# Block 1 with its late convolution tiles behind the scans, its scan tables earlier, and all four FFNs opened on three outputs

## The chip, the cores and the metric

The kernel runs on one core of a Trainium2 chip. The time is device microseconds of one execution on that core; of several executions the median is given. Within the core the engines run beside each other, each in its own fixed order of instructions: PE (matrix products), DVE (elementwise and scans), ACT (activations and casts), POOL (elementwise), SP (which issues the transfers). A wait in one engine's order holds all that stands behind it there.

## What is computed

Two blocks on 512 positions of width 1024, in float32. The first is a hybrid layer: a projection, a gated depthwise convolution of 31 taps over 1024 channels with a layer norm, beside it a state-space layer (S5), gates, an output projection. The second has two layers, each FFN, mixer, FFN; the mixer is a convolution with RWKV in the first ("even") and attention in the second ("odd").

```python
proj = einsum("bld,de->ble", rms_norm(x, pre_g), w_in)
conv_in, z_c, u_s, z_s, g_c, g_s = split(proj)
ca, cb = split(conv_in, 2)
cu = causal_depthwise_conv(ca * sigmoid(cb), conv_w, conv_b)      # 31 taps, per channel
cu = silu(layer_norm(cu, ...))
conv_out = (cu * silu(z_c)) @ w_conv_out
y = gelu(s5_mimo(u_s, ...))          # s_t = Abar s_{t-1} + Bbar u_t;  y_t = Re(C s_t) + D u_t
y = y * sigmoid(y @ w_glu + b_glu)
ssm_out = (y * silu(z_s)) @ w_ssm_out
merged = sigmoid(g_c) * conv_out + sigmoid(g_s) * ssm_out
x = x + rms_norm(merged @ w_out, post_g)
for layer in range(2):
    x = x + 0.5 * swiglu(rms_norm(x, g[0]), w_gate[layer, 0], w_up[layer, 0], w_down[layer, 0])
    x = x + (conv_rwkv if layer == 0 else attention)(rms_norm(x, g[1]))
    x = x + 0.5 * swiglu(rms_norm(x, g[2]), w_gate[layer, 1], w_up[layer, 1], w_down[layer, 1])
```

## The kernel before

**Products.** Activations lie in eight tiles of 128 channels by 512 positions. Each operand of a float32 product is split into a high and a low part, and PE does three products: high by high (L248), high weight by low activation (L249), low weight by high activation (L250). `wload` (L227) brings a weight piece of 128 by 1024: SP issues the transfer into `raw` (two buffers), ACT casts `wh` (L236, three buffers), DVE subtracts to get `wl` (L237, three buffers; POOL does it in the even mixer). `mm3` (L242) runs over the eight k tiles.

**Block 1** is a string of steps, `ORDER_A` and `ORDER_B` (L999 to L1001), which the body reads left to right. A scheduler then fixes each engine's order of instructions from that priority and from when it reckons operands to be there; class "c" is put back by 20000. A letter is a kind of step and the digit its tile or group:

- p: projection pair of a convolution tile with gating; `vb` (L699), `ca` (L701), `cu` (L708). P: the same for tiles 1, 2, 4, 6, whose convolution PE does; it writes `cp` (L720), ACT casts `cph` (L726), DVE subtracts `cpl` (L727). t: that convolution, 96 products of 256 columns (L743 to L745). c: a convolution on DVE (tiles 5 and 7, one L767 and thirty L770 each) or on POOL with ACT (tiles 0 and 3, `cw` L764 and L765).
- T: the S5 tables (`s5_tables`), some eighty small DVE operations (most by the helper at L366), a few of ACT and POOL. R: rotations (L507 to L512).
- Q, K: `s5_pre` for group q. POOL's outer products make `t1` and `w2` (L530, L533); PE transposes `t1` (L544) and multiplies `w2` (L553); SP writes `tz` row block by row block (L559). `t1` has a single buffer, so POOL's next group waits for PE's transposes; the others have two.
- q, r, x, w: `s5_main` in four parts, with the scan (L594) in the second and `sh` (L603) in the third, and PE's `py` (L608, L609) in the fourth.
- u, s, z, g: projections to u, z_s, z_c and the gates. y, G, L, S, C: gelu, GLU, layer norm (it begins with PE's sum over `sacc`, L847), the two outputs.

Tiles 5 and 7 are issued after the instruction named by `P.last_dve`, and tiles 0 and 3 after `P.last_gp`:

```python
def conv(k):
    with tc.issue_after((P.last_gp if k in CONV_POOL else P.last_dve).ins):
        conv_(k)
```

**FFN.** `ffn` (L297) runs over two halves of eleven pairs of outputs (gate and up), each from one weight load of 2048 columns, and then eight down projections. In the first FFN alone (`cols=HALVES`) the first two pairs are taken apart: three outputs are accumulated together, k by k, and the fourth follows from a weight piece of its own. The reciprocal `rs` (L286) of the norm is needed only by DVE's reading of the first output.

Of the kernel before, what the change touches and what calls it, by code (L numbers as in the profile page):

```python
# [11 lines left out]
ALU = mybir.AluOpType  # L12
PSUM = bass.MemoryType.PSUM
T = 512
# [281 lines left out]

def ffn(P, L, j, nxt, out=None, cols=()):  # L297
    nc, tc = P.nc, P.tc
    gu, dn = P.ap["ffn_gu"][L * 2 + j], P.ap["ffn_dn"][L * 2 + j]
    rs = P.rs  # L300
    P.use_banks(mm=7, sd=1)
    with tc.tile_pool(name=f"f{L}{j}", bufs=2) as ph, tc.tile_pool(name=f"m{L}{j}", bufs=1) as mp:
# [3 lines left out]
        acc = None  # L306
        first = []
        if cols:
            w0, w1 = P.wload(gu[0], 2048), P.wload(gu[1], 1024)
            pss = [P.ps() for _ in range(4)]  # L310
            for s in cols:
                for k in range(8):
                    for ps, (h, l), o in ((pss[0], w0, 0), (pss[1], w0, 1024), (pss[2], w1, 0)):
                        P.mm3(ps[:, s], h, l, o + 128 * k, [P.xh[k][:, s]], [P.xl[k][:, s]], k == 0, k == 7)
            h, l = P.wload(gu[1][:, 1024:], 1024)
            P.mm3(pss[3], h, l, 0, P.xh, P.xl)
            first = [pss[0:2], pss[2:4]]
        for hh in range(2):
            for f in range(11):
                if first:  # L320
                    pg, pu = first.pop(0)
                else:
                    h, l = P.wload(gu[hh * 11 + f], 2048)
# [27 lines left out]
def s5_tables(P, mp):  # L351
    nc = P.nc
# [49 lines left out]
    def t9(name):  # L402
        return P.t(name)[:, 0:288].rearrange("p (n g) -> p n g", n=9)

    pr, pi = t9("pr"), t9("pi")
    V.memset(pr[:, 0], 1.0)
# [51 lines left out]
    cmul(pr[:, 5:9], pi[:, 5:9], pr[:, 1:5], pi[:, 1:5], rep(pr[:, 4], 4), rep(pi[:, 4], 4), 4)  # L458
    npi, nspi, spr = small(9), t9("nspi"), small(9)
    V.tensor_scalar(out=npi, in0=pi, scalar1=-1.0, scalar2=None, op0=ALU.mult)  # L460
# [22 lines left out]
    tt(idd, P.ident[0:16, 0:16].unsqueeze(1).to_broadcast([16, 32, 16]), dd.unsqueeze(2).to_broadcast([16, 32, 16]), ALU.mult)  # L483
    prr, nspr = small(8), small(8)
    for j in range(8):
        V.tensor_copy(prr[:, j], pr[:, 7 - j])
        V.tensor_copy(nspr[:, j], nspi[:, 7 - j])
    perm = sm.tile([128, 128], F32, name="perm")
    V.tensor_copy(perm[:, 0:64], P.ident[:, 64:128])
    V.tensor_copy(perm[:, 64:128], P.ident[:, 0:64])  # L490
    return dict(bc=bc, bb=bb, bbs=bbs, idd=idd, prr=prr, nspr=nspr, spr=spr, npi=npi, mg8=mg8, rot=rot, perm=perm)


def s5_rot(P, tb):
    V = P.nc.vector
    c, s = (P.q4.tile([128, 2048], F32, name=n).rearrange("p (g k) -> p g k", g=32) for n in ("rc", "rsn"))
    V.memset(c[:, :, 0:1], 1.0)
    V.memset(s[:, :, 0:1], 0.0)
    ta, tb_ = P.t("ra"), P.t("rb")
    for i in range(6):  # L500
        m = 1 << i
        n = min(32, 512 // m)
        for g0 in range(0, 32, n):
            g = slice(g0, g0 + n)
            cq, sq = (a[:, g].unsqueeze(2).to_broadcast([128, n, m]) for a in tb["rot"][i])
            A, B = (x[:, 0:n * m].rearrange("p (g k) -> p g k", g=n) for x in (ta, tb_))
            V.tensor_tensor(out=A, in0=c[:, g, 0:m], in1=cq, op=ALU.mult)  # L507
            V.tensor_tensor(out=B, in0=s[:, g, 0:m], in1=sq, op=ALU.mult)
            V.tensor_tensor(out=c[:, g, m:2 * m], in0=A, in1=B, op=ALU.subtract)
            V.tensor_tensor(out=A, in0=s[:, g, 0:m], in1=cq, op=ALU.mult)  # L510
            V.tensor_tensor(out=B, in0=c[:, g, 0:m], in1=sq, op=ALU.mult)
            P.last_dve = V.tensor_tensor(out=s[:, g, m:2 * m], in0=A, in1=B, op=ALU.add)  # L512
    tb["cs"] = c, s


def s5_pre(P, tb, q):
    nc = P.nc
# [30 lines left out]
    for hf in range(2):  # L548
# [9 lines left out]
        for j in range(8):  # L558
            nc.sync.dma_start(tz[16 * j:16 * j + 16, 4 * hf:4 * hf + 4, 16 * j:128], kt[:, :, 0:128 - 16 * j])  # L559
    tb[q] = w2, m1, tz  # L560


def s5_main(P, tb, q, u_dram, y_dram):
# [11 lines left out]
    for j in range(8):  # L575
        nc.sync.dma_start(u[16 * j:16 * j + 16], ud[j])

# [24 lines left out]
    V.tensor_tensor(out=st3[:, :, 0:63], in0=st3[:, :, 0:63], in1=c[:, :, 0:63], op=ALU.mult)  # L602
    V.tensor_tensor(out=sh[:, :, 1:64], in0=st3[:, :, 0:63], in1=vr3[:, :, 0:63], op=ALU.subtract)  # L603
    yield
# [353 lines left out]
def proj_first(P, src, xT, sqx):  # L958
# [33 lines left out]
    for a in range(2):  # L992
# [5 lines left out]
         ("w", 1, slice(0, 512)), ("x", 3, None), ("w", 1, slice(512, 1024)), ("x", 4, None), ("x", 5, None), ("x", 6, None), ("x", 7, None))  # L998
ORDER_A = ("p0 P1 p3 t1 u0 u1 T Q0 P2 R0 K0 t2 Q1 c0 q0 K1 s0 r0 P4 x0 q1 Q2 s1 w0 r1 K2 p5 c3 x1 q2 Q3 t4 w1 r2 K3 P6 c5 "  # L999
           "x2 q3 t6 w2 r3 p7 x3 w3 c7")  # L1000
ORDER_B = "z0 z1 z2 z3 y0 g0 g1 g2 y1 y2 y3 g3 G L g4 g5 g6 S0 g7 S1 C0 C1 C2 C3 C4 C5 C6 C7"  # L1001
B1_CLASS = {"c": "C", "t": "V", "R": "T", "T": "T", "Q": "Q", "K": "Q", "q": "S", "r": "S", "x": "S", "w": "S", "y": "S", "G": "S", "L": "L"}
# [1035 lines left out]
```

## Time and profile before

| what | value |
|---|---|
| median of 3 runs | 2653.73 us (2647.78 to 2653.99) |
| the profiled execution's own time | 2650.77 us |
| its span | 2649.0 us |
| granted clock, mean | 0.97 |
| PE busy | 2512.6 us, 95% |
| DVE, ACT, POOL busy | 1474.5, 925.5, 484.2 us |
| chain that ended last | 78% PE, 9% DVE, 3% POOL |

The span is cut into stages by time: block 1 to about 560 us, the first FFN to about 955, the even mixer to about 1320, two FFNs to about 2030, the odd mixer to about 2282, the last FFN. An average over the span says little of a stage; the windows do. In a row of the windows, "PE busy" is the time in which products run, and PEclk the share of full clock that was granted. A wait row names the line that waited and the instruction that released it.

### The profile page before, as it was taken

To read this page: it belongs to the slowest core of one execution; us is meant where nothing else is said; L and a number is where in the kernel's file an instruction comes from. 1 tells how busy PE (TensorE), PEld (TensorE's weight loads), DVE (VectorE), ACT (ScalarE), POOL (GpSimd) and SP (SyncE) were. 2 spreads that over 40 slices of the span, in tenths; PEclk is the share of its full clock that TensorE was granted. 3 is DMA by queue.
4 is the path that set the end of the run, shared out by engine and by line. 5 is a ranking of instruction groups with operands and counts; after the bars stand their busy time and mean duration, and the time that the engine had idled before them with its cause. 6 is when DMAs were issued, how large, how long until landed. Compare 5 with 4: busy or idle time off the path is not lost.

```text
span 2649.0 us, 31923 instructions
## 1 busy us (share of the span) xinstructions
PE 2512.6 (95%) x12724; PEld 2052.6 (77%) x12724; DVE 1474.5 (56%) x1978; ACT 925.5 (35%) x1322; POOL 484.2 (18%) x332
## 2 busy tenths in 40 slices
PE   8687899999999998999899999999999889999999
PEld 7566788878888876787588888888888677788887
DVE  7888868455344469643754344543444766543443
ACT  5253436243222333222332233322223565422221
POOL 2499602020000164331100000100001231100000
PEclk9798899999999998998999999999999989999999
DMA  5222332313232332314132322322324412222323
GB/s 169 80 85 75 92 111 89 127 66 110 87 105 99 113 129 59 74 49 132 41 100 88 107 96 90 102 98 92 105 86 138 113 62 72 70 97 85 106 93 98
DMA packets 116294, 250.94 MB, mean 95 GB/s; under 512 B 44112, under 2 KB 53072, under 8 KB 116144
## 3 DMA queue, kind: packets, MB, share of 16 engines
q1 hardware_dynamic: 116000, 248.68, 29.7%
q8 instruction: 100, 1.64, 0.3%
q14 instruction: 50, 0.41, 0.0%
q10 hardware_dynamic: 144, 0.22, 0.0%
HBM read 234.30 MB, written 13.37 MB: 93 GB/s over the span
## 4 chain that ended last, share of the span: by engine, by line
PE 78%; DVE 9%; POOL 3%; issue 2%; DMA 2%; ACT 2%; SPq 0%; DVEq 0%; ACTq 0%; POOLq 0%
PE bank L248 24%; PE bank L249 24%; PE bank L250 24%; POOL xa L765 1%; DVE wl L237 1%; DMA s<-nd 1%; PE bank L1913 1%; DVE xa L770 1%; PE bank L1270 1%; POOL acc L265 1%; PE bank L1333 0%; ACT wh L236 0%; PE bank L1346 0%; DVE xl L271 0%; PE bank L1406 0%
## 5 line engine op out<-in xcount | busy, mean ns | idle before, releaser
L248 PE MATMUL bank<-xh,wh 128*128 128x512 f32 (+1 forms) x2152 | 836.7, 391 | 13.6 <-ACT xh L977 5.8
L236 ACT CAST wh<-raw 128x1024 fp32r<-128x1024 f32 x448 | 433.3, 968 | 1187.2 <-PE bank L249 852.5
L249 PE MATMUL bank<-xl,wh 128*128 128x512 f32 (+1 forms) x2152 | 838.0, 390 | 4.3 <-DVE xl L947 2.7
L250 PE MATMUL bank<-xh,wl 128*128 128x512 f32 (+1 forms) x2152 | 836.3, 389 | 2.7 <-DVE wl L237 2.7
L237 DVE TENSOR_TENSOR wl<-raw,wh 128x1024 fp32r<-128x1024 f32 (+2 forms) x414 | 482.7, 1166 | 331.8 <-ACT wh L236 329.3
L248 PEld LDWEIGHTS bank<-xh,wh 128*128 128x128 f32 x2152 | 406.8, 190 | 103.1 <-ACT xh L977 6.5
L249 PEld LDWEIGHTS bank<-xl,wh 128*128 128x128 f32 x2152 | 407.9, 190 | 92.1 <-DVE xl L978 4.6
L250 PEld LDWEIGHTS bank<-xh,wl 128*128 128x128 f32 x2152 | 407.8, 189 | 87.7 <-DVE wl L237 3.6
L265 POOL TENSOR_TENSOR acc<-acc,sq 128x512 f32<-128x512 f32 x54 | 90.1, 1669 | 1298.2 <-ACT sq L264 1291.6
L249 PE MATMUL bank<-ml,wh 128*128 128x512 f32 x704 | 273.9, 389 | 0.0
L250 PE MATMUL bank<-mh,wl 128*128 128x512 f32 x704 | 273.9, 389 | 0.0
L248 PE MATMUL bank<-mh,wh 128*128 128x512 f32 x704 | 272.6, 389 | 0.0
L332 DVE TENSOR_TENSOR up<-bank,rs 128x512 f32<-128x512 f32 x88 | 60.8, 691 | 271.5 <-PE bank L250 271.4
L328 DVE TENSOR_TENSOR gp<-bank,rs 128x512 f32<-128x512 f32 x88 | 60.8, 691 | 174.9 <-PE bank L250 174.7
L250 PEld LDWEIGHTS bank<-mh,wl 128*128 128x128 f32 x704 | 132.2, 188 | 27.6
L249 PEld LDWEIGHTS bank<-ml,wh 128*128 128x128 f32 x704 | 132.2, 188 | 27.4
L248 PEld LDWEIGHTS bank<-mh,wh 128*128 128x128 f32 x704 | 132.2, 188 | 27.3
L237 POOL TENSOR_TENSOR wl<-raw,wh 128x1024 fp32r<-128x1024 f32 x34 | 82.9, 2440 | 139.7 <-ACT wh L236 112.7
L765 POOL TENSOR_TENSOR xa<-xa,cw 128x512 f32<-128x512 f32 x60 | 98.0, 1635 | 10.7 <-ACT cw L764 8.1
L340 DVE SCALAR_TENSOR_TENSOR xa<-bank,xa 128x512 f32<-128x512 f32 x64 | 44.3, 692 | 79.5 <-PE bank L250 79.5
L254 ACT CAST mh<-m 128x512 fp32r<-128x512 f32 x88 | 55.1, 626 | 58.5 <-DVE m L334 58.5
L743 PE MATMUL bank<-cph,wh 128*128 128x256 f32 x128 | 41.0, 320 | 32.2 <-ACT cph L726 32.2
(654 smaller groups left out, 2927.8 us busy)
## 6 DMA issues: line engine op xcount, KB each, us to landing
raw<-in_ffn_gu_dram SPq DMA_DIRECT2D x176, 512.0 KB, 3.5
raw<-in_ffn_dn_dram SPq DMA_DIRECT2D x64, 512.0 KB, 3.5
raw<-in_w_in_dram SPq DMA_DIRECT2D x46, 512.0 KB, 3.5
raw<-in_even_in_dram SPq DMA_DIRECT2D x26, 512.0 KB, 3.5
raw<-in_ffn_dn_dram SPq DMA_DIRECT2D x64, 192.0 KB, 2.3
raw<-in_conv_dram SPq DMA_DIRECT2D x16, 512.0 KB, 3.8
xa<-in_xT_dram SPq DMA_DIRECT2D x16, 256.0 KB, 4.1
raw<-in_w_co_dram SPq DMA_DIRECT2D x8, 512.0 KB, 3.3
```

What stands on the lines that cost most here:

```text
L236: nc.scalar.copy(h[:, :m], raw[:, :m])
L237: self.wlo.tensor_tensor(out=l[:, :m], in0=raw[:, :m], in1=h[:, :m].bitcast(F32), op=ALU.subtract)
L248: self.nc.tensor.matmul(ps, h[i][:, s], xh[k], start=a, stop=False)
L249: self.nc.tensor.matmul(ps, h[i][:, s], xl[k], start=False, stop=False)
L250: last = self.nc.tensor.matmul(ps, l[i][:, s], xh[k], start=False, stop=b)
L254: self.nc.scalar.copy(hi, src)
L265: nc.gpsimd.tensor_tensor(out=acc, in0=acc, in1=sq, op=ALU.add)
L328: nc.vector.tensor_tensor(out=gp, in0=pg, in1=rs, op=ALU.mult)
L332: nc.vector.tensor_tensor(out=up, in0=pu, in1=rs, op=ALU.mult)
L340: nc.vector.scalar_tensor_tensor(out=P.x[o], in0=ps, scalar=0.5, in1=P.x[o], op0=ALU.mult, op1=ALU.add)
L743: nc.tensor.matmul(d, h[:, o], xh, start=a, stop=False)
L765: GP.tensor_tensor(out=y, in0=y, in1=w, op=ALU.add)
```

## The change

It has three parts, all in the order of work; the arithmetic and the number of transfers stay.

1. The order: T goes three steps forward, from behind u1 to before t1; P2 goes from behind Q0 to before u0, and s0, P4, t4, s1, P6 and t6 move forward among the S5 steps; and c5 and c7 go from the end of `ORDER_A` into `ORDER_B`, behind z0. `P.last_dve` is set at `sh` instead of at the last rotation, so the DVE convolutions are issued behind the last group's scan.
2. Reversed rows: the sixteen copies that made `prr` and `nspr` in reverse order (L486, L487) go. The tables are used in their own order, and `tz` and `us` are written to rows 112-16j where they went to 16j.
3. Every FFN takes the first four outputs apart; those that gave no `cols` use one slice of all 512 columns.

```diff
-def ffn(P, L, j, nxt, out=None, cols=()):
+def ffn(P, L, j, nxt, out=None, cols=(slice(0, T),)):
...
-        first = []
-        if cols:
-            w0, w1 = P.wload(gu[0], 2048), P.wload(gu[1], 1024)
-            pss = [P.ps() for _ in range(4)]
-            for s in cols:
...
+        w0, w1 = P.wload(gu[0], 2048), P.wload(gu[1], 1024)
+        pss = [P.ps() for _ in range(4)]
+        for s in cols:
+            for k in range(8):
+                for ps, (h, l), o in ((pss[0], w0, 0), (pss[1], w0, 1024), (pss[2], w1, 0)):
+                    P.mm3(ps[:, s], h, l, o + 128 * k, [P.xh[k][:, s]], [P.xl[k][:, s]], k == 0, k == 7)
+        h, l = P.wload(gu[1][:, 1024:], 1024)
+        P.mm3(pss[3], h, l, 0, P.xh, P.xl)
+        first = [pss[0:2], pss[2:4]]
...
-    pr, pi = t9("pr"), t9("pi")
+    pr, pi = small(9), t9("pi")
...
-    npi, nspi, spr = small(9), t9("nspi"), small(9)
+    npi, nspi, spr = small(9), small(9), small(9)
...
-    prr, nspr = small(8), small(8)
-    for j in range(8):
-        V.tensor_copy(prr[:, j], pr[:, 7 - j])
-        V.tensor_copy(nspr[:, j], nspi[:, 7 - j])
...
-    return dict(bc=bc, bb=bb, bbs=bbs, idd=idd, prr=prr, nspr=nspr, spr=spr, npi=npi, mg8=mg8, rot=rot, perm=perm)
+    return dict(bc=bc, bb=bb, bbs=bbs, idd=idd, prr=pr, nspr=nspi, spr=spr, npi=npi, mg8=mg8, rot=rot, perm=perm)
...
-            P.last_dve = V.tensor_tensor(out=s[:, g, m:2 * m], in0=A, in1=B, op=ALU.add)
+            V.tensor_tensor(out=s[:, g, m:2 * m], in0=A, in1=B, op=ALU.add)
...
-            nc.sync.dma_start(tz[16 * j:16 * j + 16, 4 * hf:4 * hf + 4, 16 * j:128], kt[:, :, 0:128 - 16 * j])
+            nc.sync.dma_start(tz[112 - 16 * j:128 - 16 * j, 4 * hf:4 * hf + 4, 16 * j:128], kt[:, :, 0:128 - 16 * j])
...
-        nc.sync.dma_start(u[16 * j:16 * j + 16], ud[j])
+        nc.sync.dma_start(u[112 - 16 * j:128 - 16 * j], ud[j])
...
-    V.tensor_tensor(out=sh[:, :, 1:64], in0=st3[:, :, 0:63], in1=vr3[:, :, 0:63], op=ALU.subtract)
+    P.last_dve = V.tensor_tensor(out=sh[:, :, 1:64], in0=st3[:, :, 0:63], in1=vr3[:, :, 0:63], op=ALU.subtract)
...
-ORDER_A = ("p0 P1 p3 t1 u0 u1 T Q0 P2 R0 K0 t2 Q1 c0 q0 K1 s0 r0 P4 x0 q1 Q2 s1 w0 r1 K2 p5 c3 x1 q2 Q3 t4 w1 r2 K3 P6 c5 "
-           "x2 q3 t6 w2 r3 p7 x3 w3 c7")
-ORDER_B = "z0 z1 z2 z3 y0 g0 g1 g2 y1 y2 y3 g3 G L g4 g5 g6 S0 g7 S1 C0 C1 C2 C3 C4 C5 C6 C7"
+ORDER_A = ("p0 P1 p3 T t1 P2 u0 u1 Q0 t2 R0 s0 K0 P4 Q1 c0 q0 K1 t4 r0 s1 x0 q1 Q2 p5 w0 r1 K2 P6 c3 x1 q2 Q3 t6 w1 r2 K3 p7 "
+           "x2 q3 w2 r3 x3 w3")
+ORDER_B = "z0 c5 c7 z1 z2 z3 y0 g0 g1 g2 y1 y2 y3 g3 G L g4 g5 g6 S0 g7 S1 C0 C1 C2 C3 C4 C5 C6 C7"
```

What the strings make of the engines' orders is seen in three places. The changed kernel's line numbers are lower by six in these rows (L720 is now L714), except for `wload` and `mm3`. The rows give line, operation, output, inputs and size; a count stands for rows alike.

DVE, around pair 2's `vb`. Before:

```order
L487 COPY s5t_820<-nspi 128x32 x4
L473 TENSOR_SCALAR nn<-nn 128x192
L487 COPY s5t_820<-nspi 128x32 x4
L475 SCALAR_TENSOR_TENSOR ang<-nn,ang 128x192 x2
L699 TENSOR_TENSOR vb<-bank_76,rsl 128x512
L701 TENSOR_TENSOR ca<-bank_75,rsl 128x512
L475 SCALAR_TENSOR_TENSOR ang<-nn,ang 128x192
L237 TENSOR_TENSOR wl<-raw,wh 128x1024
L720 SCALAR_TENSOR_TENSOR cp<-vb,ca 64x256 x3
```

Now:

```order
L237 TENSOR_TENSOR wl<-raw,wh 128x1024
L702 SCALAR_TENSOR_TENSOR cu<-vb,ca 128x512
L237 TENSOR_TENSOR wl<-raw,wh 128x1024 x5
L693 TENSOR_TENSOR vb<-bank_76,rsl 128x512
L695 TENSOR_TENSOR ca<-bank_75,rsl 128x512
L237 TENSOR_TENSOR wl<-raw,wh 128x1024
L714 SCALAR_TENSOR_TENSOR cp<-vb,ca 64x256 x4
L721 TENSOR_TENSOR cpl<-cp,cph 128x2x256
```

Ahead of `vb` stood the tables with their copies; now weights stand there, and the last of the tables' rows is the one just ahead of this piece.

DVE, at the convolution of tile 5 and 7. Before, around the `cp` of pair 6:

```order
L237 TENSOR_TENSOR wl<-raw,wh 128x1024
L770 SCALAR_TENSOR_TENSOR xa<-cu,hcw,xa 128x512 x3
L557 TENSOR_TENSOR kt<-kt,idd 16x4x16
L770 SCALAR_TENSOR_TENSOR xa<-cu,hcw,xa 128x512 x2
L699 TENSOR_TENSOR vb<-bank_74,rsl 128x512
L701 TENSOR_TENSOR ca<-bank_73,rsl 128x512
L770 SCALAR_TENSOR_TENSOR xa<-cu,hcw,xa 128x512
L601 TENSOR_TENSOR vr<-bank_79,rsn 128x8x63
L602 TENSOR_TENSOR st_2028<-st_2028,rc 128x8x63
L237 TENSOR_TENSOR wl<-raw,wh 128x1024
L720 SCALAR_TENSOR_TENSOR cp<-vb,ca 64x256 x4
L770 SCALAR_TENSOR_TENSOR xa<-cu,hcw,xa 128x512
```

Now, at the last group's scan and behind it:

```order
L588 SCALAR_TENSOR_TENSOR st_2383<-d_2330,vs 128x512
L237 TENSOR_TENSOR wl<-raw,wh 128x1024
L595 TENSOR_TENSOR vr<-bank_77,rsn 128x8x63
L596 TENSOR_TENSOR st_2383<-st_2383,rc 128x8x63
L597 TENSOR_TENSOR sh<-st_2383,vr 128x8x63
L761 TENSOR_SCALAR xa<-cu,hcw,vec 128x512 x2
L237 TENSOR_TENSOR wl<-raw,wh 128x1024
L764 SCALAR_TENSOR_TENSOR xa<-cu,hcw,xa 128x512 x9
```

The steps of tiles 5 and 7 were strewn through the scans and stood ahead of `cp`; now the first of them (L761) comes after the last `sh`.

PE, at the first transposes of S5 (`t` is `t1`). Before:

```order
L744 MATMUL bank_80<-cpl,wh 128x256
L745 MATMUL bank_80<-cph,wl 128x256
L743 MATMUL bank_80<-cph,wh 128x256
L744 MATMUL bank_80<-cpl,wh 128x256
L544 MATMUL bank_77<-ident,t_840 128x128 x4
L745 MATMUL bank_80<-cph,wl 128x256
```

Now:

```order
L250 MATMUL bank_74<-xh_98,wl 128x512
L248 MATMUL bank_74<-xh_99,wh 128x512
L249 MATMUL bank_74<-xl_107,wh 128x512
L250 MATMUL bank_74<-xh_99,wl 128x512
L538 MATMUL bank_77<-ident,t_898 128x128 x4
L538 MATMUL bank_78<-ident,t_898 128x128 x4
```

The first transposes, at place 418, stood inside the convolution of tile 2 (L743 to L745). They now come at place 530, behind that convolution and behind the projection s0.

## Rows read from the trace of the kernel before

**Rows 1.** Windows of block 1: span, busy time (instructions) by engine, clock, transfers.

```profile
core 0: us, PE busy (x) PEld busy (x) DVE busy (x) ACT busy (x) POOL busy (x), PEclk, DMA share, GB/s
100.00:200.00 100.00, 76.39 (x393) 63.22 (x394) 85.05 (x96) 41.51 (x59) 77.41 (x56) 0.86 0.24 72
200.00:300.00 100.00, 74.24 (x429) 63.36 (x429) 88.25 (x72) 46.30 (x68) 89.15 (x57) 0.81 0.27 78
300.00:400.00 100.00, 99.60 (x454) 82.42 (x453) 71.03 (x88) 37.98 (x51) 15.34 (x11) 1.00 0.33 105
100.00:120.00 20.00, 11.46 (x73) 11.02 (x74) 18.07 (x34) 6.42 (x9) 10.48 (x11) 0.65 0.14 40
260.00:280.00 20.00, 4.85 (x22) 4.37 (x22) 19.78 (x23) 7.45 (x12) 13.49 (x8) 0.50 0.15 42
```

**Rows 2.** PE's waits from 20 to 300 us: total, times, longest.

```profile
PE bank L743 <- ACT cph L726: 32.2, 2, 18.6
```

**Rows 3.** Timeline at the first wait: start, length, instruction [idle before it, and releaser].

```profile
79.98 0.09 DVE L406 MEMSET pr<- 128x32 f32 x1
...
98.33 2.23 DVE L487 COPY s5t<-nspi 128x32 f32<-128x32 f32 x4
...
101.94 0.68 DVE L699 TENSOR_TENSOR vb<-bank,rsl 128x512 f32<-128x512 f32 x1
...
106.18 1.28 ACT L479 ACT_TABLE_LOAD   x1 [2.90 <-DVE ang L476]
...
108.40 0.58 PE L743 MATMUL bank<-cph,wh 128*128 128x256 f32 x1 [18.61 <-ACT cph L726]
```

**Rows 4.** Timeline: a weight subtraction alone, and the second wait.

```profile
69.00 1.21 DVE L237 TENSOR_TENSOR wl<-raw,wh 128x1024 fp32r<-128x1024 f32 x1
...
268.48 2.28 DVE L237 TENSOR_TENSOR wl<-raw,wh 128x1024 fp32r<-128x1024 f32 x1
...
270.69 3.75 DVE L720 SCALAR_TENSOR_TENSOR cp<-vb,ca 64x256 f32<-64x256 f32 x4
...
275.15 0.58 PE L743 MATMUL bank<-cph,wh 128*128 128x256 f32 x1 [13.62 <-ACT cph L726]
```

**Rows 5.** Timeline of DVE beside POOL at 109.8 us.

```profile
109.76 1.27 POOL L533 TENSOR_TENSOR t<-t,tmp 128x512 f32<-128x512 f32 x1
109.80 1.28 DVE L510 TENSOR_TENSOR ra<-rsn,rc 128x32 f32<-128x32 f32 x1
```

**Rows 6.** POOL's stretch: its window, DVE's groups in it, later window of L770 alone.

```profile
117.43:255.98 138.55, 112.92 (x594) 91.79 (x592) 118.34 (x104) 59.69 (x86) 122.16 (x84) 0.91 0.27 77
...
L237 DVE TENSOR_TENSOR wl<-raw,wh 128x1024 fp32r<-128x1024 f32 x17 | 30.2, 1774 | 15.5 <-ACT wh L236 15.5
L770 DVE SCALAR_TENSOR_TENSOR xa<-cu,hcw,xa 128x512 f32<-128x512 f32 x17 | 23.6, 1386 | 0.4
...
340.00:360.00 20.00, 10.19 (x14) 1.00 0.33 109
```

**Rows 7.** Timeline: ends of POOL's stretch, and PE at place 1029 of its order.

```profile
117.43 1.26 POOL L530 TENSOR_TENSOR t<-s5bb,s5t 128x512 f32<-128x512 f32 x1 [1.04 <-PE bank L544]
...
256.04 0.40 PE L553 MATMUL bank<-w,s5bb 128*16 128x128 f32 x1 [2.71 <-POOL w L533]
...
303.33 0.39 PE L249 MATMUL bank<-xl,wh 128*128 128x512 f32 x1
303.56 0.39 PE L250 MATMUL bank<-xh,wl 128*128 128x512 f32 x1
```

**Rows 8.** Timeline of FFN openings; last row: PE's waits from 2280 to 2310 us.

```profile
592.79 0.50 PE L248 MATMUL bank<-xh,wh 128*128 128x512 f32 x1 [0.30 <-ACT wh L236]
...
1334.75 3.35 DVE L286 RECIPROCAL rs<-s 128x512 f32<-128x512 f32 x1 [1.76 <-ACT s L284]
...
PE bank L248 <- DVE xa L1952: 3.9, 1, 3.9
```

More of the change, by code (lines that the diff above doesn't have):

```diff
@@ L306, in ffn @@
         acc = None
-        first = []
-        if cols:
-            w0, w1 = P.wload(gu[0], 2048), P.wload(gu[1], 1024)
-            pss = [P.ps() for _ in range(4)]
-            for s in cols:
[L312 to L317, printed above, removed]
+        w0, w1 = P.wload(gu[0], 2048), P.wload(gu[1], 1024)
[7 more added lines that the diff above has]
+        first = [pss[0:2], pss[2:4]]
         for hh in range(2):
```

## The prediction

> **What bounds the kernel now.** I read the windows first. The reader is to see a kernel whose PE is the bound nearly everywhere, and one stretch where it isn't: from 100 to 300 us PE is busy 76.4 and 74.2 of each 100 us, at a granted clock of 0.86 and 0.81, while the 100 us behind them stand at 99.6 and 1.00 [rows 1]. The worst slices are 100 to 120 us (PE busy 11.5 of 20, clock 0.65) and 260 to 280 us (4.9 of 20, clock 0.50, the lower of the two levels, 1.2 GHz, all through). The list of PE's waits names the cause of both: ACT's cast of cph, 32.2 us in two waits, the longest 18.6 [rows 2].
>
> The timeline shows why the casts are late. First wait: DVE works from 79.98 through the S5 tables, among them small copies in POOL's company (four of 128x32 take 2.23 us), and reaches vb of pair 2 only at 101.94; its cp and cast follow, and tile 2's first product issues at 108.40 after 18.61 us of idleness [rows 3]. Second wait: at 268.48 DVE runs a weight subtraction of 2.28 us that takes 1.21 at 69.00, then four cp that take 3.75, and tile 6's first product waits for their cast until 275.15 [rows 4]. Steps of convolution tiles 5 and 7 (L770) are strewn between, in DVE's order.
>
> Both engines are slow there because they get in each other's way. At 109.80 a DVE operation on 32 columns takes 1.28 us and ends when POOL's 1.27 us one from 109.76 does [rows 5]. From 117.43 to 255.98 POOL is busy 122.2 of 138.6 us; the 17 convolution steps that DVE has there take 1386 ns each, and 0.73 us (10.19 for 14) once POOL is idle [rows 6].
>
> **What the change does, part by part.** *Tables, then P2, ahead.* In the new order the tables of T are done before t1's last weights, and pair 2's vb has six weight subtractions in front of it instead of the tables. So the wait of 18.6 us should go. The tables aren't free: they fall beside t1's weights. ACT gets four table loads of 1.28 us [rows 3] between t1's casts, 5.1 us, and I add 1.4 us for small DVE operations in front of wl: **6.5 us lost**. Bounds: nothing, if the three weight buffers cover it, or 22 us, the time from 79.98 to 101.94 that the tables take DVE now [rows 3], if they all stood in front of a weight.
>
> *When the first S5 transposes come.* PE's order stands at place 386 when the wait for pair 2 begins, 18.61 us before 108.40, at 89.8. The same 386 places hold the same work in the new order; then come t2's 96 products and the 48 of s0, and at place 530 the transposes. At 0.227 us for 512 columns (303.33 to 303.56 [rows 7]) and half of it for 256 these are 10.9 and 10.9 us: 89.8 + 21.8 + 6.5 = **118 us**, taken as 119 for the transposes themselves.
>
> *From there POOL sets the pace.* t of the S5 preparation has one buffer: POOL's outer products for q1 start at 117.43 when PE has read q0's, and PE takes q3's w at 256.04 after a wait for POOL [rows 7]. In between POOL does 73 tensor operations, 1.90 us each with its idle time. In the new order there are 82 up to the same product. Upper bound: 82 x 1.90 = 156 us. Lower: the 18 DVE steps of tiles 5 and 7 in this stretch are gone, and with them at most their own 0.73 us each in which POOL stood: 156 - 13 = 143. I take **146**, near the lower end, since the nine additional operations bring no DVE work along. So PE's last product of q3's preparation comes at 119 + 146 = 265 us. It is place 1029 of PE's new order; before, place 1029 is a projection product that issued at 303.56 [rows 7]. The new order's first 1029 places hold 3 us more PE work (by the two issue times, place by place). Gain: 303.6 + 3 - 265 = **41.6 us**. The recovered clock is in this number, as it is a difference of clock times.
>
> *The tail.* P.last_dve now lies behind q3's sh, so the 62 DVE steps of tiles 5 and 7 start only then. From there to their last one DVE has 73.6 us to do (62 x 0.73 = 45, 13 wl x 1.21 = 16, the rest z, gelu and gates); sacc adds 2.6. PE has 78 us of products between q3's py and the sum over sacc. Margin 2 us. POOL has 16 operations left after q3's w, most of them past when DVE begins, 21 us of PE work later: I take **2 us lost**. In the trace of before one POOL operation held one DVE operation for its whole length [rows 5]; if all 16 did so, 20 us less the margin would be lost, 18 instead of 2. The Trainium skill's "SBUF — State Buffer", section "SBUF: two separate sides", states this as the rule: DVE with two SBUF inputs and GpSimd lock each other out for the whole instruction. The trace agrees for that pair, and less so for the mean of 1386 ns.
>
> *The copies.* Removing 16 copies takes up to 9 us off DVE (2.23 us per four beside POOL [rows 3]). In the new place POOL has little to do, and they would cost little: nothing, beyond what the first step counts. Reversed rows of tz and us change neither number nor size of transfers: nothing.
>
> *The three FFN openings.* ffn(0,1), ffn(1,0), ffn(1,1) now start with three outputs per k, as ffn(0,0) did. There the fourth output's weight came late in three waits, the first 0.30 us [rows 8], 0.8 in all. In ffn(0,1) and ffn(1,0) DVE's new order also has the reciprocal rs in front of that weight. It starts at 1334.75 and takes 3.35 us [rows 8], some 15 after that FFN's first product, and three outputs last 72 x 0.227 = 16.3: it ends 2 us past that. So 2.8 us lost twice and 0.8 once. And ffn(1,1) opens with a wait of 3.9 us for xa [rows 8], which work on three outputs may shorten a little. I take **5 us lost**; bounds 3.9 gained and 12.4 lost (three times 0.8 + 3.35).
>
> **Sum** against the profiled run's own 2650.8 us (span 2649.0): 2650.8 - 41.6 + 2 + 5 = **2616 us**. The median of the runs is 2653.7, 3 us above; I leave the sum where it is.
>
> **Rivals.**
> 1. *POOL isn't that slow.* With less of DVE beside it POOL could need 1.55 us per operation in place of 1.78, between the 1.27 undisturbed [rows 5] and the 122.2/73 = 1.67 busy [rows 6]. q3's preparation ends 18 us earlier: **2598**. Against: weights (1774 ns [rows 6]), rotation and scans stay there.
> 2. *The tables starve t1.* Should all 22 us stand in front of t1's weights, 15.5 more are lost than counted, and POOL starts as much later: **2631**. For it: the tables are serial over DVE and ACT, and both run in order. Against: the order has seven weight subtractions among them.
> 3. *POOL's last operations hold DVE in the tail.* All 16 of them cost 18 instead of 2: **2632**. It is what the lock rule in the Trainium skill's "SBUF — State Buffer" makes of the tail. Against: 17 steps at 1386 ns are less than 0.73 + 1.27 each, so not every step met one.
> 4. *The tail becomes DVE's; slower.* All 62 steps at the 1386 ns that they took beside POOL are 41 us more, the 13 weights at 1774 ns 7 more: 46 past the margin. PE waits for gates and the sum, and loses to the clock what 100 to 120 us shows, 7 of 20, twice. 2650.8 - 41.6 + 46 + 14 + 5 = **2674**. It decides if POOL is at tile 3 through most of the 62 steps, that is if ACT starves POOL or q3's w comes well before sh. Against: 16 operations at 1.67 are 27 us, no more.
> 5. *The change doesn't do what it says:* pair 2's cast is late all the same, because vb waits for its banks or for tanh's table. The first wait stays with its slow clock, 18.6 + 7: **2642**.
>
> **How the numbers follow.** A measurement here tells about 0.3%, 8 us, from no change. Chances: forecast 0.45 (2606 to 2626), rival 1 0.14, rivals 2 and 3 0.12 each, rival 5 0.05, rival 4 0.07, and 0.05 for what I don't see, most of it slower. Range 2592 to 2642: it takes in rivals 1, 2, 3 and 5 and the bounds of the openings around the forecast, and leaves out 4. Faster by over 0.3% (under 2646): 0.83; within: 0.06; slower: 0.11.
>
> **What would show it.** Right: no wait of L743 for cph over 2 us; PE above 17 of 20 us and clock above 0.95 in the slices from 80 to 240; PE's remaining waits on POOL's w and t; q3's last product of the preparation at about 265; no L770 before q3's sh; DVE above 90% from there; gaps of 1 to 3 us some 16 us after each FFN's first product. Wrong: PE waiting for wl or wh between 45 and 80 us (rival 2), for gates, z or sacc between 290 and 370 (3, 4), for cph at 100 (5). The forecast fails as a whole if the time is above 2646, or if the gain lies outside block 1.

## The result, and the profile after

The changed kernel takes 2629.34 us (median of 3 runs, 2629.21 to 2631.49) where the one before took 2653.73: a ratio of 0.9922, with a 95% interval of 0.9903 to 0.9942. The forecast was 2616 within 2592 to 2642. The profiled execution is the run of 2629.34 us, with a span of 2627.6 and a mean clock of 0.973; against the profiled 2650.77 before, the gain is 21.4 us where 34.8 were forecast. From the S5 rotations on, line numbers of the new kernel are 6 lower (L770 is L764, L743 is L737); the helpers up to L286 keep theirs.

PE's waits in the new kernel, 20 to 420 us (total, times, longest):

```profile
PE bank L737 <- ACT cph L720: 11.6, 2, 7.7
PE bank L739 <- DVE wl L237: 5.2, 3, 3.6
PE bank L738 <- DVE cpl L721: 5.0, 3, 2.3
PE bank L547 <- ACT vs L579: 4.2, 1, 4.2
PE bank L547 <- POOL w L527: 3.0, 1, 3.0
...
PE bank L248 <- DVE zc L793: 1.6, 1, 1.6
```

The wait for cph, 32.2 us in two [rows 2], is down to 11.6, and the first of the two, 18.6 us long, is gone altogether: the two that are left are at tiles 4 and 6. In its place stand many small ones. The windows of the new kernel show where:

```profile
core 0: us, PE busy (x) PEld busy (x) DVE busy (x) ACT busy (x) POOL busy (x), PEclk, DMA share, GB/s
40.00:60.00 20.00, 14.09 (x69) 12.43 (x68) 19.79 (x30) 5.68 (x13) 14.38 (x11) 0.84 0.16 51
100.00:120.00 20.00, 20.00 (x135) 18.50 (x134) 15.69 (x34) 8.28 (x10) 1.73 (x4) 1.00 0.59 183
140.00:160.00 20.00, 8.96 (x41) 6.68 (x41) 16.72 (x13) 7.89 (x13) 19.92 (x13) 0.56 0.24 66
220.00:240.00 20.00, 8.32 (x47) 7.61 (x48) 12.06 (x9) 6.54 (x10) 18.76 (x13) 0.69 0.14 38
260.00:280.00 20.00, 20.00 (x108) 15.94 (x106) 11.46 (x10) 10.70 (x16) 19.45 (x16) 1.00 0.26 74
```

The two bad slices of before [rows 1] are full now: 20.00 of 20 at a clock of 1.00 where 11.46 at 0.65 and 4.85 at 0.50 stood. Two new bad slices lie at 40 to 60, where the tables are made, and at 140 to 160 (8.96 of 20 at a clock of 0.56, where the kernel before had 14.60 at 0.91). One is left at 220 to 240, where POOL is busy 18.76 of 20 us and DVE only 12.06. The timeline of the new kernel shows the waits of the second slice and of the third, at tile 6, and the end of the S5 preparation (start, length, instruction, idle before it and releaser):

```profile
142.30 0.57 ACT L549 COPY kt<-bank 16x512 f32<-16x512 f32 x1 [8.40 <-DMA tz<-kt]
...
143.02 1.09 PE L538 MATMUL bank<-ident,t 128*128 128x128 f32 x4 [2.41 <-ACT kt L549]
...
148.27 3.57 PE L547 MATMUL bank<-w,s5bb 128*16 128x128 f32 x16 [4.16 <-ACT vs L579]
...
155.72 0.58 PE L737 MATMUL bank<-cph,wh 128*128 128x256 f32 x1 [3.88 <-ACT cph L720]
...
223.05 0.72 ACT L758 ACTIVATE cw<-cu,hcw 128x512 f32<-128x512 f32 x1 [5.76 <-POOL xa L759]
223.68 1.03 ACT L236 CAST wh<-raw 128x1024 fp32r<-128x1024 f32 x1
224.62 0.63 ACT L694 ACTIVATE vb<-vb 128x512 f32<-128x512 f32 x1
...
224.74 1.65 DVE L237 TENSOR_TENSOR wl<-raw,wh 128x1024 fp32r<-128x1024 f32 x1 [4.20 <-ACT wh L236]
226.32 5.52 DVE L714 SCALAR_TENSOR_TENSOR cp<-vb,ca 64x256 f32<-64x256 f32 x4
...
232.54 0.58 PE L737 MATMUL bank<-cph,wh 128*128 128x256 f32 x1 [7.72 <-ACT cph L720]
...
266.92 1.41 POOL L527 TENSOR_TENSOR w<-w,tmp 128x576 f32<-128x576 f32 x1
...
270.32 1.05 PE L547 MATMUL bank<-w,s5bb 128*16 128x128 f32 x8
```

In the slice at 140 PE waits three times for ACT: 2.41 us for a copy of `kt` that ACT makes only after 8.40 us of waiting for the transfer of `tz`, 4.16 for `vs` and 3.88 for the cast of tile 4. At tile 6 too the chain runs over ACT, which works in order. At 223.05 it makes the next `cw` of tile 3 only after 5.76 us of waiting for POOL; a weight cast and the gate `vb` of tile 6's pair stand behind that. DVE waits 4.20 us for the cast, its four `cp` take 5.52 beside POOL (3.75 before [rows 4]), and PE's product waits for all of it. The marks that the forecast used, in us:

| mark | before | after | shift | forecast shift |
|---|---|---|---|---|
| first S5 transposes on PE | 115.1 | 124.1 | +9.0 | +4 |
| the two products that the forecast took for place 1029 of PE's order | 303.6 | 270.3 | -33.2 | -38.6 |
| sum over sacc (layer norm) | 409.8 | 380.9 | -28.9 | -39.6 |
| rs of ffn(0,0) | 603.7 | 575.3 | -28.4 | -39.6 |
| rs of the even mixer | 948.9 | 921.3 | -27.6 | |
| rs of ffn(0,1) | 1334.8 | 1315.1 | -19.6 | -37 |
| rs of ffn(1,0) | 1690.6 | 1671.3 | -19.3 | |
| rs of the odd mixer | 2050.5 | 2032.9 | -17.6 | |
| rs of ffn(1,1) | 2299.0 | 2276.6 | -22.4 | -34.8 |
| end | 2650.8 | 2629.3 | -21.4 | -34.8 |

The second row doesn't compare one place. Counted as the forecast counts (the first transposes are number 418 before and 530 after), the product at 303.6 is number 1222 of the profiled order of the kernel before, and the last of q3's preparation, at 271.1, is number 1192 of the new one; number 1192 of the kernel before issues at 296.8.

What block 1 gained can be split by the windows from 20 us to the sum over sacc: PE's idle time falls from 60.0 to 37.3 us, and its busy time from 329.8 to 323.6 at a clock that rises from 0.91 to 0.94. Of the 28.9 us 22.7 are waits.

So two things fell short: block 1 gains 28 us and not 40, and the even mixer loses 8 us, in a stage that the change doesn't touch. The odd mixer gives 5 back. The experiments below ask what makes the 28, why it isn't more, and where the 8 went.

### The profile page after: what moved, and what is told of

It is laid out like the page before. It is cut to its first block, busy times and chain, and to the rows that moved or that the text cites. A ratio compares the mean times of both kernels' runs of the same rounds, so it can differ in the third digit from the quotient of the medians.

```text
span 2627.6 us, 31906 instructions
## 1 busy us (share of the span) xinstructions
PE 2513.7 (96%) x12724; PEld 2054.1 (78%) x12724; DVE 1449.1 (55%) x1962; ACT 928.9 (35%) x1325; POOL 477.6 (18%) x332
## 4 chain that ended last, share of the span: by engine, by line
PE 81%; DVE 9%; POOL 3%; DMA 2%; ACT 2%; issue 2%; SPq 1%; DVEq 0%; POOLq 0%; ACTq 0%
PE bank L248 24%; PE bank L250 24%; PE bank L249 24%; DVE wl L237 1%; POOL xa L759 1%; DMA raw<-in_w_in_dram 1%; POOL acc L265 1%; PE bank L1907 1%; PE bank L1264 1%; ACT wh L236 1%; SPq L553 1%; PE bank L1340 0%; PE bank L1327 0%; DMA s<-nd 0%; DVE cp L714 0%
## 5 line engine op out<-in xcount | busy, mean ns | idle before, releaser
L248 PE MATMUL bank<-xh,wh 128*128 128x512 f32 (+1 forms) x2152 | 836.4, 390 | 16.9 <-ACT xh L971 6.0
L248 PEld LDWEIGHTS bank<-xh,wh 128*128 128x128 f32 x2152 | 405.9, 189 | 108.6 <-issue 7.5
L248 PE MATMUL bank<-mh,wh 128*128 128x512 f32 x704 | 272.6, 389 | 0.0
L248 PEld LDWEIGHTS bank<-mh,wh 128*128 128x128 f32 x704 | 132.2, 188 | 27.5
L332 DVE TENSOR_TENSOR m<-up,sg 128x512 f32<-128x512 f32 x88 | 60.9, 692 | 10.5 <-ACT sg L328 2.3
```

Source lines behind the costliest of these rows:

```text
L248: self.nc.tensor.matmul(ps, h[i][:, s], xh[k], start=a, stop=False)
```

## Experiments

The kernel before was run beside each group of experiments on the same chip; its medians were 2649.96 (beside block 1 alone, FFNs alone, early convolutions, late tables), 2651.17 (copies, tile 6, tile 3, tiles 0 and 3) and 2649.43 (the rest). "Low stretch" is the time that the even mixer spends at a clock under 0.9 around its triangular solve, counted in windows of 2 us; it is 18 us in the kernel before and 36 in the new one.

**Which of the three parts.** The block 1 part alone (the FFNs as before), and the FFN part alone:

```diff
-def ffn(P, L, j, nxt, out=None, cols=(slice(0, T),)):
+def ffn(P, L, j, nxt, out=None, cols=()):
...
```

> The changed kernel with the FFNs of before (only the first one opens on three outputs). Theory: the three new openings are worth next to nothing, since in the changed kernel's trace the second and third FFN differ from before by 1.4 and 0.6 us and the last by no wait at all. So 2627 to 2631 us against 2629. Block 1 keeps its 28 us, and the even mixer its stretch at half clock near 1190 us, because its order of work is the changed kernel's. Rival, as forecast: the openings cost 5 us, then 2624. Second rival: an opening is what shortened the odd mixer's wait for ACT (13.2 to 9.6 us); then 2633.

Measured: 2626.69 us (2625.83 to 2629.20), 0.9913 of before (0.9898 to 0.9928).

> The kernel before with all FFNs opened on three outputs, nothing else. Theory: within 2 us of before, 2651 to 2656, the even mixer with the order of before and the short stretch at half clock (16 us, not 32). Rival: openings cost 5 us, 2658. Second rival: they gain 4 us through the odd mixer, 2649.

Measured: 2651.25 us, 1.0006 of before (0.9996 to 1.0015). The FFN openings are worth nothing: +1.3 us alone, up to 2.6 together with the rest. All of the gain is in block 1.

**The late convolutions.** Tiles 5 and 7 go back to their places between the S5 steps, all else as in the new kernel:

```diff
-            V.tensor_tensor(out=s[:, g, m:2 * m], in0=A, in1=B, op=ALU.add)
+            P.last_dve = V.tensor_tensor(out=s[:, g, m:2 * m], in0=A, in1=B, op=ALU.add)
...
-    P.last_dve = V.tensor_tensor(out=sh[:, :, 1:64], in0=st3[:, :, 0:63], in1=vr3[:, :, 0:63], op=ALU.subtract)
+    V.tensor_tensor(out=sh[:, :, 1:64], in0=st3[:, :, 0:63], in1=vr3[:, :, 0:63], op=ALU.subtract)
...
-ORDER_A = ("... w1 r2 K3 p7 x2 q3 w2 r3 x3 w3")    ORDER_B = "z0 c5 c7 z1 ..."
+ORDER_A = ("... w1 r2 K3 c5 p7 x2 q3 w2 r3 x3 w3 c7")    ORDER_B = "z0 z1 ..."
```

> The changed kernel with one part undone: the DVE convolutions may start after the last rotation again, c5 stands behind K3 and c7 at the end of the first string. Theory (POOL sets the pace of the S5 preparation and DVE's two-input work slows it): POOL's stretch from the first transposes to q3's w goes from 1.75 us per operation back to 1.9, 8 to 13 us, and pair 6's cast is late again, so 2638 to 2645. Rival (the tail is what counts: DVE is busy 105.5 of 112.9 us there): the work spread out is better, 2625 or less. Second rival (POOL does not pace PE): no change, 2629.

Measured: 2657.89 us (2654.69 to 2663.57), 1.0034 of before (1.0022 to 1.0045): slower than the kernel before, and 29 us behind the new one. Its waits of PE, 20 to 420 us, and then its windows:

```profile
PE bank L737 <- ACT cph L720: 18.2, 2, 14.3
PE bank L591 <- DVE st L588: 9.2, 1, 9.2
PE bank L739 <- DVE wl L237: 8.6, 4, 3.5
PE bank L547 <- POOL w L527: 5.8, 2, 5.3
```

```profile
220.00:240.00 20.00, 5.50 (x24) 4.52 (x24) 19.82 (x17) 4.29 (x7) 18.86 (x12) 0.60 0.16 43
240.00:260.00 20.00, 11.80 (x74) 11.30 (x74) 19.68 (x18) 8.39 (x12) 16.85 (x10) 0.71 0.12 34
300.00:320.00 20.00, 10.79 (x45) 7.96 (x43) 19.75 (x20) 3.88 (x5) 10.38 (x7) 0.82 0.18 47
```

DVE is full (19.7 to 19.8 of 20) and PE empty. The DVE steps and what they cost beside POOL, 120 to 300 us of this run (count, busy, mean ns), against the same operation late in the new kernel, 294 to 390 us:

```profile
L764 DVE SCALAR_TENSOR_TENSOR xa<-cu,hcw,xa 128x512 f32<-128x512 f32 x32 | 43.7, 1367 | 0.7
```

```profile
L764 DVE SCALAR_TENSOR_TENSOR xa<-cu,hcw,xa 128x512 f32<-128x512 f32 x60 | 43.0, 754 | 0.0
```

The same step takes 1367 ns beside POOL and 754 ns after it. The mean mixes two kinds (shortest, median and longest of the 32, in ns):

```profile
L764 DVE SCALAR_TENSOR_TENSOR xa<-cu,hcw,xa x32: 730/1636/1878, 208.1 to 298.7; 128x512 f32<-128x512 f32 x32
```

Ten of them take 730 to 752 ns and 22 take 1470 to 1878, with none between, and each of the 22 ends 0.50 to 0.55 us after a POOL operation does. The two other parts of the new order (tables ahead, no copies) gain nothing while the convolutions stay early.

**The tables.** T goes back behind u1:

```diff
-ORDER_A = ("p0 P1 p3 T t1 P2 u0 u1 Q0 ..."
+ORDER_A = ("p0 P1 p3 t1 P2 u0 u1 T Q0 ..."
```

> The changed kernel with T behind u1 again, everything else kept. Theory (POOL's pace counts from the first transposes on): the waits of 7.5 us and the lower clock (0.84 from 40 to 60 us) in tile 1's convolution vanish, about 10 us, but the tables then run at 80 to 105 us and POOL has q0's products ready only at about 120, where the transposes would have been anyway: 2624 to 2631. Rival (PE alone limits from there): the full 10 us are gained, 2619. Second rival (the tables stand in front of pair 2's operands as before): the wait of 18 us is back, 2645 or more.

Measured: 2636.81 us (2633.95 to 2637.66), 0.9951 (0.9934 to 0.9967). The sum over sacc comes at 393.8, 13 us later than in the new kernel; the total shows only 7.5 of that, since the stage of the low stretch is 8.0 us shorter (16 us at the low clock instead of 36). The first product of tile 2's convolution issues at 89.9 us, where it is 101.8 in the new kernel: that is what tables ahead cost PE up to there. The wait of 18.6 us doesn't come back. In this order P2 still stands ahead of the tables, so the wait goes with P2's place and not with the tables' own (P2 alone was not moved in any run). The delay spreads over waits of 11.0 us (L547 for ACT's `vs`), 7.8 (`zc`), 7.5 (L547 for ACT's `m`) and 6.5 (cph). So tables ahead are worth some 13 us in block 1, net of what they cost t1.

**The copies.** The 16 copies and forward rows come back:

```diff
+    prr, nspr = small(8), small(8)
+    for j in range(8):
+        V.tensor_copy(prr[:, j], pr[:, 7 - j])
+        V.tensor_copy(nspr[:, j], nspi[:, 7 - j])
...
-            nc.sync.dma_start(tz[112 - 16 * j:128 - 16 * j, 4 * hf:4 * hf + 4, 16 * j:128], kt[:, :, 0:128 - 16 * j])
+            nc.sync.dma_start(tz[16 * j:16 * j + 16, 4 * hf:4 * hf + 4, 16 * j:128], kt[:, :, 0:128 - 16 * j])
...
```

> The changed kernel with the sixteen copies and the forward rows back. Theory: in the new place POOL has little to do and the copies cost 0.1 to 0.2 us each on DVE, 2 to 3 us, of which tile 1's weights see at most that: 2628 to 2633. Rival: they lengthen the wait for tile 1's low parts (7.5 us now), and with it all that follows: 2636 or more.

Measured: 2631.49 us (2623.68 to 2634.39), 0.9914 (0.9894 to 0.9934): the same as the new kernel in total, and 6 us later at the end of block 1 (rs of ffn(0,0) at 581.3 against 575.3); the stage of the low stretch, 22 us instead of 36, gives 4.4 of them back. In the trace of this run the copies fall in POOL's company again:

```profile
51.52 2.16 DVE L485 COPY s5t<-nspi 128x32 f32<-128x32 f32 x4
...
54.85 2.31 DVE L485 COPY s5t<-nspi 128x32 f32<-128x32 f32 x3
```

**Is POOL what sets the pace?** Tiles 0 and 3 get half of their further taps; that work is left out.

```diff
-                for j in range(1, 31):
+                for j in range(1, 16):
```

> The changed kernel with half of POOL's convolution left out (tiles 0 and 3 take 15 of their 30 further taps; ACT's scaled copies for them go too). Nothing is moved into the tail, unlike with tiles 3 and 0 late. Theory (POOL sets the pace up to q3's w, and ACT's casts wait behind ACT's copies for POOL): 20 to 30 of the 82 operations go, the two casts' waits of 11.6 us shrink, PE reaches place 1029 some 25 us sooner than at 270 us and the time is 2600 to 2612. Rival (the S5 chain over PE, ACT and DVE paces itself): place 1029 comes 10 us sooner at most, as with tile 3 late, 2618 to 2625.

Measured: 2614.5 us (2 runs), 0.9867 (0.9848 to 0.9887). Between 120 and 270 us POOL has 30 of these additions (47.5 us) instead of 49 (76.1 us), 28.6 us less, and the end of the preparation comes only 8.7 us sooner (262.4 against 271.1), the sum over sacc 8.9. Most of the rest of the gain in the total, 6.1 us, lies in the stage of the low stretch, 22 us instead of 36, of which more below. POOL stands idle instead. Its row at 200 us, and the window ahead of it, in this run:

```profile
200.06 0.95 POOL L541 MEMSET tz<- 128x1024 f32 x1 [13.63 <-PE bank L602]
```

```profile
180.00:200.00 20.00, 20.00 (x112) 17.08 (x111) 11.07 (x12) 7.65 (x9) 6.19 (x4) 1.00 0.33 106
```

From 180 to 200 PE is full and POOL waits 13.63 us for it; the wait for cph is 12.1 us, as in the new kernel. So POOL isn't the only pace: of the work taken from it a third shows. The run with tiles 0 and 3 late, below, says the same more strongly: from the first transposes to q3's last product POOL is busy 57.8 us instead of 133.6, and the stretch still takes 125.5 us instead of 147.0. PE's own work and the chain of S5 steps over PE, ACT and DVE hold the rest.

**Tile 6 moved behind K3**, so that its cast has time:

```diff
-"... K2 P6 c3 x1 q2 Q3 t6 w1 r2 K3 p7 "
+"... K2 P6 c3 x1 q2 Q3 w1 r2 K3 t6 p7 "
```

> The changed kernel with the convolution of tile 6 moved behind the last group's preparation. PE waits 7.7 us for its cast and 2.1 for its low part at 232 us, at a clock of 0.69. Theory (POOL sets the pace up to q3's w at 268 us): that wait is slack that POOL leaves anyway; PE will wait for POOL's products instead, 2625 to 2633. Rival (the casts are what PE loses on): the wait goes, with its clock some 14 us, 2615.

Measured: 2626.7 us (2620.62 to 2631.06), 0.9904 (0.9884 to 0.9923). cph is waited for 5.0 us instead of 11.6, but sacc comes only 2.3 sooner (378.6). The waits are not made up elsewhere: up to the sum over sacc PE is idle 27.6 us where it was 37.3 in the new kernel. It is busy 331.0 us where it was 323.6. The slice at tile 6's old place, in this run, shows where the busy time grew:

```profile
220.00:240.00 20.00, 16.65 (x71) 14.22 (x69) 16.52 (x13) 8.34 (x13) 17.72 (x13) 0.51 0.12 35
```

PE is busy 16.65 of 20 us instead of 8.32, but at a clock of 0.51: the wait is gone and 7.4 of the 9.7 us go into slower products.

**More convolutions late.** Tile 3, and then tiles 0 and 3 (both POOL's), join tiles 5 and 7 in the tail:

```diff
-"... P6 c3 x1 q2 ..."    ORDER_B = "z0 c5 c7 z1 ..."
+"... P6 x1 q2 ..."    ORDER_B = "z0 c3 c5 c7 z1 ..."
```

> The changed kernel with POOL's convolution of tile 3 behind z0 as well, so that it no longer stands among the outer products. Theory (POOL sets the pace): 17 of the 82 operations between the first transposes and q3's w go, 17 x 1.75 = 30 us, PE reaches place 1029 some 25 to 30 us sooner; the 30 steps then lie beside DVE's 62 in the tail and slow them, 20 us of DVE work, of which 10 to 15 past PE's margin: 2612 to 2622. Rival (the casts on ACT and DVE set the pace): q3's w comes sooner but PE doesn't, and the tail costs 10 to 15: 2640.

Measured: 2633.21 us (2628.33 to 2634.48), 0.9927 (0.9912 to 0.9941). The preparation ends at 259.7 (11.4 sooner), the sum over sacc at 388.5 (7.6 later).

> The same with tile 0 late too: no convolution step of POOL is left among the outer products. Theory: PE becomes the bound up to place 1029, which it reaches at about 220 us instead of 270; 60 POOL steps then run beside 62 DVE steps, DVE's take 1.39 us each instead of 0.73, and the tail is DVE's by some 40 us: 2615 to 2630. Rival (no lock worth the name in the tail): the 50 us stay, 2580. Second rival (casts set the pace): no gain and a slow tail, 2650 or more.

Measured: 2652.62 us (2646.47 to 2657.94), 1.0004 (0.9990 to 1.0017): the whole gain is gone. The preparation ends at 248.3, 22.8 us sooner; the sum over sacc at 403.4, 22.5 later. The windows of this run between them, and its two largest waits of PE:

```profile
320.00:340.00 20.00, 15.73 (x61) 11.91 (x59) 20.00 (x18) 9.46 (x16) 12.62 (x8) 0.91 0.21 66
340.00:360.00 20.00, 13.06 (x48) 10.31 (x48) 20.00 (x18) 11.39 (x18) 13.32 (x9) 0.83 0.16 53
360.00:380.00 20.00, 14.45 (x54) 11.08 (x55) 20.00 (x18) 7.86 (x11) 12.65 (x8) 0.91 0.19 58
```

```profile
PE bank L250 <- DVE wl L237: 16.8, 6, 5.4
PE bank L248 <- DVE zc L793: 8.5, 1, 8.5
```

DVE is busy 20.00 of 20 us beside POOL's 13, does 18 instructions per slice, and PE falls to 13 to 16. This is the mechanism that the fourth rival described: it exists, and it decides the time where POOL runs beside the 62 steps.

**The loss in the even mixer.** In the new kernel its order is another one, since a scheduler fixes it from when it reckons operands to be there, and block 1's end has moved. The class "F2", the products of the convolution's output, is put 50 sooner:

```diff
-EV_PRIO = {..., "B1": 1000, "F2": 1600, ...}
+EV_PRIO = {..., "B1": 1000, "F2": 1550, ...}
```

> The changed kernel with one number altered in the even mixer: the output projection's products (128 by 512, the fillers there) get priority 1550 instead of 1600. In PE's order twelve of them then stand between the small products of the triangular solve near 1185 us, where the changed kernel has none until 1196. Theory (the clock falls to half in the wait and rises again only after a run of the large products): the stretch at half clock goes from 36 us to 20 or less, and the time from 2629 to 2619 to 2623. Rival (DVE's chain sets that stage, the clock only fills it): no change, 2629. Second rival: fillers taken here are missing later, the loss moves to the next wait, 2626 to 2630.

Measured: 2617.35 us (2611.78 to 2621.25), 0.9877 (0.9860 to 0.9893), 12 us ahead of the new kernel. First the new kernel's windows there, then this run's:

```profile
1170.00:1180.00 10.00, 8.40 (x72) 6.80 (x71) 2.75 (x6) 1.04 (x1) 2.35 (x1) 0.83 1.06 190
1180.00:1190.00 10.00, 9.57 (x120) 9.31 (x120) 6.41 (x13) 1.17 (x2) 0.00 (x0) 0.50 0.40 154
1190.00:1200.00 10.00, 10.00 (x87) 8.71 (x86) 2.67 (x4) 0.72 (x2) 1.04 (x1) 0.50 0.26 80
1200.00:1210.00 10.00, 10.00 (x66) 7.86 (x65) 0.69 (x1) 1.09 (x3) 1.04 (x1) 0.50 0.14 41
1210.00:1220.00 10.00, 10.00 (x99) 8.03 (x98) 1.37 (x2) 3.90 (x8) 2.37 (x1) 0.96 0.53 168
```

```profile
1170.00:1180.00 10.00, 9.36 (x46) 6.86 (x46) 3.31 (x7) 1.05 (x1) 4.28 (x2) 1.00 1.04 210
1180.00:1190.00 10.00, 9.93 (x158) 8.78 (x158) 6.83 (x13) 1.68 (x3) 0.21 (x1) 1.00 0.82 236
1190.00:1200.00 10.00, 10.00 (x123) 8.32 (x119) 4.36 (x7) 1.25 (x3) 3.37 (x2) 1.00 0.58 168
```

In the new kernel the clock falls to 0.50 where PE has gaps (8.40 of 10 busy at 1170), and stays there past 1200, though PE is busy 9.57 to 10.00 of 10 meanwhile; it does only 66 to 120 products per 10 us. In this run products of 512 columns (`L248 cr,wh`) fill most of 1170 to 1180 and 1186.6 to 1189.3, between the solve's products of 64 rows, and the clock stays at 1.00 with 123 to 158 products. The time from rs of ffn(0,0) to rs of ffn(0,1) rises with the low stretch through the fourteen kernels; ten of them:

| run | low stretch | rs to rs |
|---|---|---|
| F2 sooner | 0 us | 724.9 us |
| tile 3 late | 12 | 728.9 |
| tables late | 16 | 731.8 |
| before | 18 | 731.1 |
| copies back | 22 | 735.5 |
| half of POOL's taps | 22 | 733.7 |
| tiles 0 and 3 late | 24 | 736.8 |
| block 1 alone | 28 | 737.1 |
| new kernel | 36 | 739.8 |
| t6 later | 40 | 739.7 |

The order of work in this stage explains only part of it. By the traces the kernel with the copies back has in the even mixer the same order of instructions as the new kernel, on PE, DVE, ACT and POOL, and its low stretch is 22 us and not 36. Tile 3 late has the same order as tiles 0 and 3 late (12 and 24 us), and tables late the same as half of POOL's taps (16 and 22). So one order comes with different low stretches, and the new order with copies back is 4.4 us behind the kernel before where the new kernel is 8.8. What sets the rest was not found; each row is one traced execution.

**Together.** Block 1's part with FFNs as before and F2 sooner, and the same with tile 6 behind K3; the edits are those above.

> The same number altered in the version that keeps the FFNs of before (block 1's change alone, 2626.7 so far, 28 us at half clock). Theory: 5 us from the clock, 2619 to 2623. Rival: no change, 2627.

Measured: 2613.24 us (2610.52 to 2619.76), 0.9866 (0.9852 to 0.9881).

> The same with tile 6's convolution behind the last group's preparation too (2 us in block 1, by its trace). Theory: 2617 to 2622, the fastest of all. Rival: tile 6's move is worth nothing in a median, as the whole run with it alone showed (2626.7 against 2629), and it equals the one before.

Measured: 2613.64 us (2608.67 to 2615.97), 0.9858 (0.9841 to 0.9874). Both beat both kernels, by 36 us the one before and by about 15 the changed one; between the two there is no difference, though tile 6 was worth 2 us in block 1.

Not tried: two buffers for `t1`, which would let POOL's next group start before PE's transposes.

## Why the prediction was right, and where it was off

- **The wait of 18.6 us goes: right**, and with it the clock of 0.65; the slice at 100 to 120 is full. The run with the tables late points to P2's place ahead of them as what does it.
- **What the tables cost t1: 6.5 us forecast, about 12 found.** PE waits 2.3, 3.6, 0.9 and 0.7 us in t1 (48.8 to 66.4 us), 7.5 in all, and the clock falls to 0.84 in that slice. Tile 2's first product issues at 101.8, where 89.8 without a cost was counted on. The step missed that POOL's first outer products follow the tables at once, at 46 us, so the small table operations meet POOL there as they did in their old place. The transposes come at 124.1 and not 119.
- **The copies, "nothing": wrong for the same reason.** They would have cost 6 us in block 1; "in the new place POOL has little to do" did not hold.
- **POOL's stretch, 146 us from the transposes to q3's last product: 146.2 found (147.0 to the very last), by luck.** Its reason, "from there POOL sets the pace", holds only in part: taking 28.6 us of work from POOL moved the end by 8.7, so the rate of before already had PE, ACT and DVE in it. The signs that were named fail with it. PE is idle 27.6 us in that stretch, and the profile puts only 4.6 of them down to POOL itself (3.0 for `w`, 1.6 for `d`), the others to ACT and DVE. The slices at 140, 200 and 220 are under 17 of 20 us, and the wait for cph is 7.7 and 3.9 us where none over 2 was to be left.
- **"3 us more PE work" in the first 1029 places: the sign was wrong.** From its mark to the sum over sacc the new kernel has 108.8 us of PE work in 110.6, the one before 105.8 in 106.2. So the new order has 3 us less done at the mark, and part of what was gained there is paid behind it. The two marks are 30 products apart in the profiled orders (numbers 1222 and 1192). Block 1 is 10.7 us short at sacc: 5 by the late transposes, 6 by this sign.
- **The tail, 2 us lost: right.** PE is idle 1.8 us there (1.6 for `zc`) where it was 0.4 before, and the steps take 754 ns. The lock rule of the Trainium skill's "SBUF — State Buffer", section "SBUF: two separate sides", by which a DVE instruction with two SBUF inputs and a GpSimd instruction that reads SBUF block each other for the whole instruction, was weighed there. The forecast read the mean of 1386 ns as agreeing less with it than the pair. The single steps of the run with the convolutions early agree with it: they take either 730 to 752 ns or 1470 to 1878, and every long one ends 0.50 to 0.55 us after a POOL operation. So each step fits the rule as the pair does, and the mean only says how many were held.
- **The FFN openings, 5 us lost: about 0 to 2.6**, inside the bounds.
- **Nothing outside block 1: wrong.** The forecast counted no change in the even mixer; from rs of ffn(0,0) to rs of ffn(0,1) 8.8 us were lost, with 18 us more at the low clock. The order there shifted with block 1's, but with the same order and the copies back the loss is 4.4, so the order alone doesn't explain it, and what else does stays open. The odd mixer's stretch gave 5 back, 243.7 us where it was 248.5. The other twelve traces have 244.3 to 249.6 there, with and without the new openings, and no run asked why.
- **The rivals.** The measured time lies between the forecast's own band (2606 to 2626) and rivals 2 and 3 (2631 and 2632). Rival 2 came true in part: its sign, PE waiting for `wl` between 45 and 80 us, is there (5.2 us), and the transposes are late by 5 of its 15.5 us. Rival 3's sign is hardly there: between 290 and 370 us PE waits 1.6 us for `zc` and for nothing else. That the tail becomes DVE's was shown possible by putting POOL's tiles late; in the change as it stands it doesn't happen. That POOL isn't that slow didn't come true, and the wait of rival 5 is gone. The late convolutions carry the gain: without them the kernel is slower than before.

The total, 2629, lies in the range because the direction and the large term were right, and because the range was drawn wide enough to take in rivals 2 and 3. Of the 13.4 us between it and the forecast 11.2 are block 1's. Behind it 7.0 were lost (8.8 in the even mixer's stretch, 3.0 in the FFNs, less 4.8 in the odd mixer) where 5 were forecast, for another reason.

## What to carry to other kernels

Before pricing an engine as the pace of a stretch, look for what the others would wait for if it were faster: taking 28.6 us of work from POOL was worth 8.7. A wait that is taken away isn't all gain either: with tile 6 later 9.7 us of idle time went and 2.3 us were won, since the products then ran at a clock of 0.51. Vector work that shares a stretch with GpSimd costs nearly twice in the mean (1367 against 754 ns); put it where GpSimd is idle and PE has enough queued, and no more of it than fits. When a scheduler sets the order, a change in one stage can reorder later ones, and the same order can come out 4 us apart: compare marks stage by stage, and look at the granted clock of stages that nobody touched.

## What the runs showed of the hardware

A busy PE isn't always a PE at full clock. In the even mixer the clock stayed at 0.50 (1.2 GHz) for 36 us while the profile has PE busy 9.57 to 10.00 of 10 us, mostly with small products (32 or 64 rows and columns); with more products of 512 columns ahead of them and among them it did not fall in that stretch. The same order of instructions came with 36 us at the low level in one kernel and 22 in another. Fourteen kernels range from 0 to 40 us at the low level and from 724 to 740 us for the stage: 15 us, beside the 21 that the change gained in all.

Beside POOL the DVE convolution steps, with two tiles as inputs, were either free (10 of 32, 730 to 752 ns) or held (22, 1470 to 1878 ns), and each that was held ended 0.50 to 0.55 us after a POOL operation.
